# A static list schedule that counts the SBUF port of VectorE and GpSimd once, in a two-layer encoder kernel

## The chip, the cores and the metric

The kernel runs on one core of one Trainium2 chip. The metric is device time in microseconds (us); the kernel before takes 1868.65 us, the median of three runs (1866.95 to 1869.14).

## The reference

Two inputs, `x_prompt` (512 tokens) and `x_sample` (256 tokens), both 1024 wide, go through two layers of the same trunk. Cut to what matters:

```python
for l in range(2):
    h = rms_norm(x, norm_mix[l]);  proj = h @ w_in[l]          # q: 16 heads, k and v: 8 heads, 64 wide
    o_a = dense attention, 4 heads, axial rotary positions
    o_b = neighbourhood attention, 6 heads: a query sees up to 8 rows x 16 columns of the token grid,
          with a learned bias per head
    o_c = dilated attention, 6 heads, three branches merged by their softmax sums
    y = concat(rms_norm(o_a), rms_norm(o_b), rms_norm(o_c)) * out_gain[l]
    x = x + y @ w_out[l]
    gate, up = split(rms_norm(x, norm_ffn[l]) @ w_gate_up[l])  # 2 x 2816 wide
    x = x + (silu(gate) * up) @ w_down[l]
```

## The kernel before, in words

All 768 tokens stay in SBUF, feature-major, as blocks of 128. `p` counts three pairs of blocks: 0 and 1 are the prompt, 2 is the sample. Every float32 operand of a large product is split into a rounded part (`wh`, `Tph`, ...) and the difference to it (`wl`, `Tpl`, ...); `mm3` (L498 to L500) then makes three matmuls in place of one. A weight piece (`Piece`) is loaded by SP into one of two `raw` tiles, rounded by ScalarE into `wh` (L473), and the difference goes to `wl` (L474). Which engine does the difference is said by the parameter `wlo`, which is `POOL` in both layers. There are four `wh`/`wl` pairs.

A layer has an attention stage and an FFN stage. In the attention stage, for each of eight head groups `g` (the three of the neighbourhood mixer, m = 1, come first, then the dilated ones, m = 2, then the dense ones, m = 0), `emit_qkv` makes q, k and v (norms and rotary positions are small elementwise work on DVE and POOL, L661 to L704; L712 and L716 transpose the result), and `emit_attn` does, for each pair of blocks and each of two heads: scores (L781), bias and minimum (L826), exponential (L829), transposes of the probabilities (L840), rounding (L865) and difference (L866) of the transposed probabilities, product with the values (L876), and evacuation (L885, L890). `emit_out` scales by the output norm (L938 to L941) and projects. The residual add is L965. `norm2` (with `root`, L504 to L523) and `split` (L529, L532) prepare the FFN.

In the neighbourhood mixer the prompt's probabilities lie in a tile of 384 columns, three blocks of keys. A block of queries uses 256 of these; the rest is set to zero by `pads` on POOL (L820, L822). All three key blocks are transposed, rounded and multiplied for both query blocks, the blocks of zeros too.

The order of the instructions on each engine is no hand-written list. Every operation is recorded in a `Plan` with an engine (or several to choose from), a cost in us and a priority; `Plan.emit` simulates the engines with these costs and writes the instructions out in the order that comes from it. Each engine then works its list strictly in order, so a late instruction holds up those behind it. Among several engines one is passed over when another would finish over `TOL` = 0.7 us sooner. Costs before: an elementwise operation of n columns takes 0.07 + n/960 on DVE and 0.155 + 0.0021 n on POOL, whatever the other of the two does; a matmul takes its columns over 2400. Waits are set from the data, so the costs change the order alone.

```python
        def start_time(o, e):
            s = max(clock[e], o.ready)
            ...
    ew(width, lambda E: E.tensor_tensor(self.flat(1), raw[0][:, :width], self.flat(0).bitcast(F32), op=OP.subtract),
       r=[raw] + w[0], w=w[1], prio=prio, on="wlo")
```

Of the kernel before, what the change touches and what calls it, by code (L numbers as in the profile page):

```python
# [8 lines left out]
F32 = mybir.dt.float32  # L9
# [31 lines left out]
     qw=-8.0, qp2=-1.0, wlo='POOL', sth='ACT', rot='DVE POOL', cos='DVE POOL', radd='POOL', qsc='DVE POOL',  # L41
     stl='DVE POOL', qcp='ACT', kcp0='DVE', kcp1='ACT', kcp2='ACT', bias='POOL', pth='ACT', ysq='POOL', yadd='POOL', alo='DVE',
     nsq='ACT', nadd='DVE', nhi='ACT DVE', nlo='POOL', yhl='DVE POOL', tout=0, tdn=1, n1=2, nf=86, gus=-1, sf=5, wide=(), om=1,
# [6 lines left out]
     qw=-8.0, qp2=0, wlo='POOL', sth='ACT', rot='POOL', cos='DVE POOL', radd='POOL', qsc='DVE POOL', stl='DVE POOL',  # L50
     qcp='ACT', kcp0='DVE', kcp1='ACT', kcp2='ACT', bias='DVE POOL', pth='ACT', ysq='POOL', yadd='POOL', alo='POOL', nsq='ACT',
     nadd='DVE POOL', nhi='ACT DVE', nlo='POOL', yhl='DVE POOL', tout=0, tdn=1, n1=2, nf=86, gus=-1, sf=5, wide=(), om=1,
# [20 lines left out]
class Op:  # L73
    __slots__ = ("eng", "cost", "fn", "prio", "ndep", "outs", "ready", "alloc", "bufs", "end", "lat", "start", "seq", "bytes", "opts", "rank")


class Plan:
# [36 lines left out]
    def op(self, eng, cost, fn, r=(), w=(), prio=0.0, after=(), lat=0.0, nbytes=0):  # L114
        o = Op()
        o.opts = {eng: (cost, fn)} if isinstance(eng, str) else {e: (c, f) for e, c, f in eng}
        o.eng = next(iter(o.opts))
        o.cost, o.fn = o.opts[o.eng]
        o.prio, o.lat, o.bytes = prio, lat, nbytes
        o.seq = len(self.ops)  # L120
        o.alloc, o.bufs, o.outs, o.ready = [], set(), [], 0.0
        deps = set(after)
        for t in list(r) + list(w):
            b = t if isinstance(t, Buf) else (t[0] if isinstance(t, tuple) and isinstance(t[0], Buf) else None)
            if b is not None and b not in o.bufs:
                o.bufs.add(b)
                b.left += 1
                if b.first is None:
                    b.first = o
                    o.alloc.append(b)  # L130
                else:
                    deps.add(b.first)
        for t in r:
            if t in self.writer:
                deps.add(self.writer[t])
            self.readers.setdefault(t, []).append(o)
        for t in w:
# [12 lines left out]

    def emit(self):
# [59 lines left out]
        while left:  # L211
# [24 lines left out]
            o.cost, o.fn = o.opts[e]  # L236
# [7 lines left out]
            o.start = s  # L244
            clock[o.eng] = s + o.cost
# [28 lines left out]
def trunk(ctx: ExitStack, tc: tile.TileContext, t):  # L274
# [96 lines left out]
    def dve(n, fn, r=(), w=(), prio=0.0, fast=False):  # L371
        return P.op("DVE", v_cost(n, fast), fn, r, w, prio, lat=0.05)
# [6 lines left out]
    def ew(n, fn, r=(), w=(), prio=0.0, on="DVE POOL", act=None, fast=False, ptr=False, sbuf=True, extra=0):  # L379
# [9 lines left out]
        return P.op(opts, 0.0, None, r, w, prio, lat=0.05)  # L389
# [7 lines left out]
    TR = 0.108  # L397
# [104 lines left out]
    def root(parts, n, prio, exact, rb, out, to):  # L502
# [6 lines left out]
        else:  # L509
# [4 lines left out]
                r=[tok, (sh, 0)], w=[(sh, 1)], prio=prio)  # L514
# [5 lines left out]
            pe(2 * 0.108, total, r=[(sh, 0), (sh, 1), "ones"], w=[pm, (rb, "hold")], prio=prio)  # L520
# [113 lines left out]
    def emit_qkv(l, g, bs, wp, gains, rope):  # L634
# [6 lines left out]
        for p in order(g):  # L641
            acc = P.buf("D")
            av = lambda acc=acc: acc[0].rearrange("p (j c) -> p j c", j=2)
            for j in range(2):
                for kk in range(0, KC, 2):
# [5 lines left out]
                    pe(6 * 0.108, mm, r=[x for x in pc[kk // 4].tokens if len(x) == 2 or x[2] == kk // 2 % 2] + [x for x in pc[1].tokens if kk == 0 and len(x) == 2] + [  # L651
# [67 lines left out]
            pe(4 * 0.056, trq, r=[(stk, 0), (stk, 1), "identr"], w=[pq], prio=pr)  # L719
            ew(512, lambda E, p=p, pq=pq: E.tensor_copy(query(gs, p), pq[0]), r=[pq], w=[(gs[p], "q", p)], prio=pr, on="qcp",  # L720
               act=lambda p=p, pq=pq: ACT.copy(query(gs, p), pq[0]), sbuf=False)
            pe(2 * 0.056, trk, r=[(stk, 0), (stk, 1), "identr"], w=[pk], prio=pr)
# [9 lines left out]
    def emit_attn(l, g, gs, bs, mc):  # L732
# [15 lines left out]
        for p in order(g):  # L748
# [11 lines left out]
            wide = (g, p) in K["wide"]  # L760
# [6 lines left out]
            for h in range(2):  # L767
                PP = []
                for j in range(2):
# [14 lines left out]
                    pe(2 * nk / 2400.0, qk, r=[(gs[p], "q", p)] + ktok, w=[S], prio=pr)  # L784
# [13 lines left out]
                    else:  # L798
# [33 lines left out]
                for c in range(0, nch, 2):  # L832
                    n = min(2, nch - c)
                    pt = P.buf("PT")

                    def tr(c=c, n=n, pt=pt, PP=PP):
                        v = pt[0].rearrange("p (c j t) -> p c j t", c=2, j=2)
                        for cc in range(n):
                            for j in range(2):
                                PE.transpose(v[:, cc, j], PP[j][0][:, (c + cc) * 128:(c + cc + 1) * 128], ident)  # L840

                    rr_ = PP + ([(a, 1) for a in PP] if m == 1 and p < 2 else [])
                    pe(2 * n * TR, tr, r=rr_ + ["ident"], w=[pt], prio=pr)
                    vt = [(gs[pp], "v", pp, i) for pp in ((0, 1) if p < 2 else (2,)) for i in range(2)]
                    if wide:
                        for cc in range(n):
                            sr = lambda cc=cc, pt=pt: pt[0][:, cc * 256:(cc + 1) * 256]
                            ds = lambda c=c, cc=cc, PP=PP: PP[cc][0][:, c * 128:c * 128 + 256]
                            ew(256, lambda E, sr=sr, ds=ds: E.tensor_copy(ds(), sr()), r=[pt], w=[(PP[cc], "t", c)], prio=pr,
                               sbuf=False, on="pth", act=lambda sr=sr, ds=ds: ACT.copy(ds(), sr()))  # L850

                        def pv(c=c, n=n, h=h, p=p, po=po, nch=nch, c0=c0, PP=PP):
                            for cc in range(n):
                                kb = c0 + c + cc
                                pp, jj = (kb // 2, kb % 2) if p < 2 else (2, c + cc)
                                v = vals(gs, pp)[:, jj].bitcast(F32)
                                PE.matmul(po[0][:, h * 256:(h + 1) * 256], v, PP[cc][0][:, c * 128:c * 128 + 256],
                                          start=c + cc == 0, stop=c + cc == nch - 1)

                        pe(4 * n * 0.108, pv, r=[(PP[cc], "t", c) for cc in range(n)] + vt, w=[po], prio=pr)  # L860
                        continue
                    ps_ = P.buf("PTS")
                    ew(256 * n, lambda E, n=n, pt=pt, ps_=ps_: E.tensor_copy(ps_[0][:, :256 * n], pt[0][:, :256 * n]), r=[pt],
                       w=[(ps_, 0)], prio=pr, sbuf=False, on="pth",
                       act=lambda n=n, pt=pt, ps_=ps_: ACT.copy(ps_[0][:, :256 * n], pt[0][:, :256 * n]))  # L865
                    dve(256 * n, lambda n=n, pt=pt, ps_=ps_: DVE.tensor_tensor(  # L866
                        ps_[1][:, :256 * n], pt[0][:, :256 * n], ps_[0][:, :256 * n].bitcast(F32), op=OP.subtract),
                        r=[pt, (ps_, 0)], w=[(ps_, 1)], prio=pr)

                    def pv(c=c, n=n, ps_=ps_, h=h, p=p, po=po, nch=nch, c0=c0):  # L870
                        for cc in range(n):
                            kb = c0 + c + cc
                            pp, jj = (kb // 2, kb % 2) if p < 2 else (2, c + cc)
                            v = vals(gs, pp)[:, jj]
                            for i in range(2):
                                PE.matmul(po[0][:, h * 256:(h + 1) * 256], v, ps_[i][:, cc * 256:(cc + 1) * 256],  # L876
                                          start=(c + cc == 0 and i == 0), stop=(c + cc == nch - 1 and i == 1))

                    pe(2 * n * 0.108, pv, r=[(ps_, 0), (ps_, 1)] + vt, w=[po], prio=pr)
# [33 lines left out]
    def emit_out(l, m, bs):  # L913
# [6 lines left out]
        for p in order(LAST[m]):  # L920
# [22 lines left out]
            for cp in range(4):  # L943
                acc = P.buf("D")
                for j in range(2):
# [7 lines left out]
                    pe(3 * n * 0.108, mm, r=[x for c in pc for x in c.tokens] + [(y, z) for y in yts for z in range(2)], w=[acc],  # L953
# [15 lines left out]
    def emit_ffn(l, base, ends, late):  # L969
        f0 = 0  # L970
        lastsilu = None
        for part, nf in enumerate(FPARTS):
            pb_ = base + part * 20
            ab = []
            for f in range(f0, f0 + nf):
# [9 lines left out]
                for s in ((1, 0) if K["gus"] < 0 and part == 0 and f < 2 else (0, 1)):  # L985
# [4 lines left out]
                    for u in range(2):  # L990
                        for kk in range(0, KC, 2):
# [5 lines left out]
                            pe(6 * n / 2400.0, mm, r=pc[kk // 4].tokens + [  # L997
# [31 lines left out]
            if part < len(FPARTS) - 1:  # L1029
                for c in range(KC):  # L1030
# [3 lines left out]
                    for s in range(2):  # L1034
                        n = 512 if s == 0 else 256
                        for i in range(nf):
# [4 lines left out]
                            pe(3 * n / 2400.0, mm, r=pc.tokens + [(ab[i], 0, s), (ab[i], 1, s)], w=[accs[s]], prio=pd)  # L1041
# [4 lines left out]
            else:  # L1046
# [4 lines left out]
                for p in range(3):  # L1051
                    s, o = (0, p * 256) if p < 2 else (1, 0)
                    for cp in range(4):
                        acc = P.buf("ANY")
                        for j in range(2):
# [5 lines left out]
                            pe(3 * nf * 0.108, mm, r=pcs[cp].tokens + [(a, z, s) for a in ab for z in range(2)], w=[acc],  # L1061
# [132 lines left out]
```

## Time and profile before

| | us |
|---|---|
| median of three runs | 1868.65 |
| the profiled execution, its own time | 1867.04 |
| its span, first to last instruction | 1865.3 |
| PE busy | 1803.0 |
| DVE busy | 817.3 |
| ACT busy | 767.0 |
| POOL busy | 830.7 |

The time outside the span is 1.7 us. Engines: PE is TensorE (PEld its weight loads), DVE VectorE, ACT ScalarE, POOL GpSimd, SP SyncE, which issues the DMAs. A matmul counts as busy from its issue to the modelled end, and matmuls overlap, so the rate of matmuls is read from the distances of their starts. The attention stages lie at about 47 to 403 us and 925 to 1326 us of the span, the FFN stages behind each of them.

### The profile page before, as it was taken

To read this page: it belongs to the slowest core of one execution; us is meant where nothing else is said; L and a number is where in the kernel's file an instruction comes from. 1 tells how busy PE (TensorE), PEld (TensorE's weight loads), DVE (VectorE), ACT (ScalarE), POOL (GpSimd) and SP (SyncE) were. 2 spreads that over 40 slices of the span, in tenths; PEclk is the share of its full clock that TensorE was granted. 3 is DMA by queue.
4 is the path that set the end of the run, shared out by engine and by line. 5 is a ranking of instruction groups with operands and counts; after the bars stand their busy time and mean duration, and the time that the engine had idled before them with its cause. 6 is when DMAs were issued, how large, how long until landed. Compare 5 with 4: busy or idle time off the path is not lost.

```text
span 1865.3 us, 30054 instructions
## 1 busy us (share of the span) xinstructions
PE 1803.0 (97%) x12008; PEld 1648.0 (88%) x12008; DVE 817.3 (44%) x1678; ACT 767.0 (41%) x1738; POOL 830.7 (45%) x711
## 2 busy tenths in 40 slices
PE   6999999989999999999998999998999999999999
PEld 5998999878888888888998999998888888888889
DVE  8788678762111211211668876877411111111112
ACT  5887586642112212212457765866421122122120
POOL 4775354343333433433435653543454354355342
PEclk8999999999999999999998999999999999999999
DMA  4321111112211221122222211101212222122212
GB/s 147 84 57 46 35 44 37 35 46 63 63 60 66 60 76 57 55 73 67 69 59 59 61 35 35 53 24 35 68 49 66 68 63 60 60 68 60 69 58 86
DMA packets 56892, 110.61 MB, mean 59 GB/s; under 512 B 24496, under 2 KB 29616, under 8 KB 56752
## 3 DMA queue, kind: packets, MB, share of 16 engines
q1 hardware_dynamic: 56752, 108.69, 19.0%
q8 instruction: 94, 1.54, 0.3%
q14 instruction: 46, 0.38, 0.1%
HBM read 105.52 MB, written 3.15 MB: 58 GB/s over the span
## 4 chain that ended last, share of the span: by engine, by line
PE 84%; DVE 9%; ACT 3%; issue 2%; DMA 1%; POOL 1%; SPq 0%; DVEq 0%; POOLq 0%; ACTq 0%
PE ps L498 25%; PE ps L499 25%; PE ps L500 25%; PE ps L876 3%; PE ps L781 3%; PE ps L840 2%; DVE Tpl L532 1%; PE ps L712 1%; DVE rp L866 1%; DVE stk L704 1%; DVE y L938 1%; ACT wh L473 0%; DVE p L826 0%; DVE Tsl L532 0%; PE ps L902 0%
## 5 line engine op out<-in xcount | busy, mean ns | idle before, releaser
L474 POOL TENSOR_TENSOR wl<-raw,wh 128x1024 fp32r<-128x1024 f32 (+1 forms) x186 | 421.4, 2268 | 557.2 <-ACT wh L473 556.3
L473 ACT CAST wh<-raw 128x1024 fp32r<-128x1024 f32 (+1 forms) x186 | 184.4, 992 | 510.7 <-PE ps L499 499.7
L499 PE MATMUL ps<-Tpl,wh 128*128 128x512 f32 x704 | 278.4, 395 | 1.1 <-DVE Tpl L532 1.1
L498 PE MATMUL ps<-Tph,wh 128*128 128x512 f32 x704 | 278.5, 396 | 0.0
L500 PE MATMUL ps<-Tph,wl 128*128 128x512 f32 x704 | 274.1, 389 | 0.0
L500 PE MATMUL ps<-Tsh,wl 128*128 128x256 f32 x704 | 199.4, 283 | 0.0
L499 PE MATMUL ps<-Tsl,wh 128*128 128x256 f32 x704 | 199.2, 283 | 0.0
L498 PE MATMUL ps<-Tsh,wh 128*128 128x256 f32 x704 | 198.3, 282 | 0.0
L1004 DVE TENSOR_TENSOR p<-ps,bt 128x256 f32<-128x256 f32 x88 | 35.9, 420 | 344.5 <-PE ps L500 331.2
L498 PE MATMUL ps<-wh,Tph 128*128 128x256 f32 x512 | 152.1, 297 | 9.6 <-ACT wh L469 8.8
L500 PEld LDWEIGHTS ps<-Tph,wl 128*128 128x128 f32 x704 | 132.6, 188 | 30.2
L499 PE MATMUL ps<-wl,Tph 128*128 128x256 f32 x512 | 146.9, 287 | 3.0 <-DVE wl L470 2.9
L498 PEld LDWEIGHTS ps<-Tph,wh 128*128 128x128 f32 x704 | 133.8, 190 | 17.7
L499 PEld LDWEIGHTS ps<-Tpl,wh 128*128 128x128 f32 x704 | 133.8, 190 | 16.7 <-DVE Tpl L532 1.4
L500 PE MATMUL ps<-wh,Tpl 128*128 128x256 f32 x512 | 146.4, 286 | 0.0
L498 PEld LDWEIGHTS ps<-Tsh,wh 128*128 128x128 f32 x704 | 133.9, 190 | 14.1
L499 PEld LDWEIGHTS ps<-Tsl,wh 128*128 128x128 f32 x704 | 133.9, 190 | 12.6
L1009 POOL TENSOR_TENSOR p<-p,p 128x512 f32<-128x512 f32 (+1 forms) x88 | 89.4, 1016 | 105.9 <-DVE p L1004 89.3
L1004 DVE TENSOR_TENSOR p<-ps,cs 128x512 f32<-128x512 f32 x88 | 60.4, 687 | 169.6 <-PE ps L500 169.1
L500 PEld LDWEIGHTS ps<-Tsh,wl 128*128 128x128 f32 x704 | 133.9, 190 | 0.0
L498 PE MATMUL ps<-yt,wh 128*128 128x256 f32 (+1 forms) x448 | 132.3, 295 | 0.0
L499 PE MATMUL ps<-yt,wh 128*128 128x256 f32 (+1 forms) x448 | 130.6, 292 | 0.9 <-DVE yt L941 0.8
(243 smaller groups left out, 4542.6 us busy)
## 6 DMA issues: line engine op xcount, KB each, us to landing
raw<-in_w_gu SPq DMA_DIRECT2D x88, 512.0 KB, 3.6
raw<-in_w_down SPq DMA_DIRECT2D x48, 384.0 KB, 3.1
raw<-in_w_in SPq DMA_DIRECT2D x32, 512.0 KB, 3.8
raw<-in_w_out SPq DMA_DIRECT2D x16, 512.0 KB, 3.8
raw<-in_w_down SPq DMA_DIRECT2D x8, 512.0 KB, 3.6
tbm<-in_rpb SPq DMA_DIRECT2D x96, 24.0 KB, 2.2
tbm<-in_rpb SPq DMA_DIRECT2D x48, 48.0 KB, 2.3
out_y<-xp SPq DMA_DIRECT2D x8, 256.0 KB, 2.1
```

The costliest lines, as they stand in the source:

```text
L473: act(width, lambda: ACT.copy(self.flat(0), raw[0][:, :width]), r=[raw], w=w[0], prio=prio)
L474: ew(width, lambda E: E.tensor_tensor(self.flat(1), raw[0][:, :width], self.flat(0).bitcast(F32), op=OP.subtract), r=[raw] + w[0], w=w[1], ...
L498: PE.matmul(out, a[0], b[0], start=start, stop=False)
L499: PE.matmul(out, a[0], b[1], start=False, stop=False)
L500: PE.matmul(out, a[1], b[0], start=False, stop=stop)
L532: ew(256, lambda E, k=k, g=g, p=p: E.scalar_tensor_tensor(tT(p, 1)[:, k], xT(p)[:, k], g, tT(p, 0)[:, k].bitcast(F32), op0=OP.mult, op1=OP ...
L704: ew(384, lambda E, rv=rv, stk=stk: E.tensor_tensor(stk[0][:, :, 1], rv(), stk[0][:, :, 0].bitcast(F32), op=OP.subtract), r=[(A, 1), (stk, ...
L781: PE.matmul(S[0][:, :nk], q, kk[:, k0:k0 + nk], start=i == 0, stop=i == 1)
L840: PE.transpose(v[:, cc, j], PP[j][0][:, (c + cc) * 128:(c + cc + 1) * 128], ident)
L876: PE.matmul(po[0][:, h * 256:(h + 1) * 256], v, ps_[i][:, cc * 256:(cc + 1) * 256], start=(c + cc == 0 and i == 0), stop=(c + cc == nch - ...
L1004: dve(n, lambda n=n, u=u, s=s, sg=sg, view=view: DVE.tensor_tensor(sg[u][:, :n], view(u), late[s][0][:, :n], op=OP.mult), r=[accs[u % len( ...
L1009: ew(n, lambda E, n=n, sg=sg: E.tensor_tensor(sg[1][:, :n], sg[0][:, :n], sg[1][:, :n], op=OP.mult), r=[(sg, 0)], w=[(sg, 1), sg], prio=pb ...
```

## The change

- `Plan.emit` keeps the time to which DVE and POOL hold a common port. A POOL operation starts no earlier than the port is free of DVE; a DVE operation marked `lock` (its operands all in SBUF) no earlier than the port is free of POOL. Both book it for their own cost. Operations of `ew` are marked by `sbuf`, one more in `root` by hand; a DVE operation that reads PSUM is not marked.
- The planned times of matmuls change: 0.0135 us is added to n/2400, 0.120 stands for 256 columns, 0.109 for a float32 transpose and 0.067 for a rounded one.
- `wlo` becomes `POOL DVE`: either engine may make a weight difference.
- In the neighbourhood mixer, prompt pairs, the key block that holds zeros alone for one query block is left out for that block (`grps`): one transpose, half of a rounding, half of a difference, and half the columns of two matmuls fewer for each head and pair. One of the three memsets goes with it; the others' priority falls by 1.
- A variant that no layer used (`wide`) is removed.

```diff
-     qw=-8.0, qp2=-1.0, wlo='POOL', sth='ACT', ...
+     qw=-8.0, qp2=-1.0, wlo='POOL DVE', sth='ACT', ...
...
+        port = {"DVE": 0.0, "POOL": 0.0}
+
+        def held(o, e):
+
+            if e == "POOL":
+                return port["DVE"]
+            return port["POOL"] if e == "DVE" and o.lock else 0.0
+
         def start_time(o, e):
-            s = max(clock[e], o.ready)
+            s = max(clock[e], o.ready, held(o, e))
...
             o.start = s
+            o.cost = o.opts[e][0]
+            if e == "POOL" or (e == "DVE" and o.lock):
+                port[e] = s + o.cost
...
-        return P.op(opts, 0.0, None, r, w, prio, lat=0.05)
+        return P.op(opts, 0.0, None, r, w, prio, lat=0.05, lock=sbuf)
...
-    TR = 0.108
+    TR = 0.109
...
-                    pe(6 * 0.108, mm, r=...)
+                    pe(6 * 0.120, mm, r=...)
...
+                        if p < 2 and p != j:
                             def pads(pr_=pr_, w0=w0, nk=nk, ncols=ncols):
-                                if w0 > 0:
-                                    POOL.memset(pr_[0][:, 0:w0], 0.0)
-                                if w0 + nk < ncols:
-                                    POOL.memset(pr_[0][:, w0 + nk:ncols], 0.0)
-
-                            P.op("POOL", 0.2, pads, r=[(gs[p], "q", p)], w=[(pr_, 1)], prio=pr - 1, lat=0.05)
+                                POOL.memset(pr_[0][:, 0:w0], 0.0)
+                                POOL.memset(pr_[0][:, w0 + nk:ncols], 0.0)
+
+                            P.op("POOL", 0.3, pads, r=[(gs[p], "q", p)], w=[(pr_, 1)], prio=pr, lat=0.05)
...
+                grps = [((c, c + 1), (0, 1)) for c in range(0, nch - 1, 2)]
+                if m == 1 and p < 2:
+                    grps = [((p, p + 1), (0, 1)), ((2 - 2 * p,), (1 - p,))]
+                for gi, (cs, js) in enumerate(grps):
+                    n = 128 * len(cs) * len(js)
...
+                    def pv(cs=cs, js=js, ps_=ps_, ...):
+                        wd = 128 * len(js)
+                        o = h * 256 + js[0] * 128
...
+                                PE.matmul(po[0][:, o:o + wd], v, ps_[i][:, z * wd:(z + 1) * wd], ...)
```

## Rows read from the trace of the kernel before

**Rows 1.** Busy time by stage: us, then busy (count) of each engine, granted clock.

```profile
core 0: us, PE busy (x) PEld busy (x) DVE busy (x) ACT busy (x) POOL busy (x), PEclk, DMA share, GB/s
0.00:47.00 47.00, 28.89 (x182) 27.93 (x183) 37.86 (x64) 24.38 (x57) 19.84 (x24) 0.89 0.44 147
47.00:403.00 356.00, 336.90 (x2685) 323.34 (x2684) 276.31 (x601) 247.94 (x652) 191.90 (x213) 0.99 0.17 49
403.00:925.00 522.00, 521.88 (x3021) 459.69 (x3019) 115.04 (x201) 118.72 (x175) 195.08 (x113) 1.00 0.21 64
925.00:1326.00 401.00, 379.87 (x2982) 363.59 (x2983) 307.81 (x666) 265.46 (x696) 187.39 (x207) 0.98 0.15 44
```

**Rows 2.** Waits of PE, whole span: us in total, times, longest.

```profile
PE ps L567 <- ACT yt L558: 6.2, 2, 5.7
...
PE ps L712 <- DVE stk L704: 3.7, 4, 1.2
...
PE ps L781 <- DVE g1a L726: 2.5, 1, 2.5
```

**Rows 3.** Timeline of POOL and DVE, 39 to 47 us: start, us, instruction.

```profile
39.55 0.56 DVE L704 TENSOR_TENSOR stk<-ppa,stk 128x384 fp32r<-128x384 f32 x1 [0.24 <-ACT stk L703]
...
45.77 2.39 POOL L474 TENSOR_TENSOR wl<-raw,wh 128x1024 fp32r<-128x1024 f32 x1 [4.33 <-ACT wh L473]
...
46.13 2.44 DVE L704 TENSOR_TENSOR stk<-ppa,stk 128x384 fp32r<-128x384 f32 x1 [0.15 <-ACT stk L703]
```

**Rows 4.** Timeline around 400 us, end of layer 0's attention stage.

```profile
396.90 4.83 POOL L474 TENSOR_TENSOR wl<-raw,wh 128x1024 fp32r<-128x1024 f32 x2
...
397.42 2.12 DVE L513 TENSOR_TENSOR yt<-tbm,yt 128x256 fp32r<-128x256 f32 x1 [1.27 <-ACT yt L512]
...
402.07 0.58 PE L518 MATMUL ps<-yt,ones 128*128 128x256 f32 x1 [3.95 <-DVE yt L513]
```

**Rows 5.** Timeline of PE, POOL and DVE around 990 us, layer 1.

```profile
990.25 1.64 PE L876 MATMUL ps<-rp,g0b 128*128 128x256 f32 x4 [3.30 <-DVE y L890]
...
992.71 2.68 POOL L474 TENSOR_TENSOR wl<-raw,wh 128x1024 fp32r<-128x1024 f32 x1
...
993.09 2.68 DVE L810 TENSOR_TENSOR bt<-tbm,maskb 128x256 f32<-128x256 f32 x1
...
996.77 1.00 PE L876 MATMUL ps<-rp,g0b 128*128 128x256 f32 x3 [1.51 <-DVE rp L866]
```

**Rows 6.** Timeline of DVE and POOL, start of the kernel.

```profile
23.39 7.39 DVE L532 SCALAR_TENSOR_TENSOR Tsl<-xs,gcol,Tsh 128x256 fp32r<-128x256 f32 x5
...
25.61 4.89 POOL L474 TENSOR_TENSOR wl<-raw,wh 128x1024 fp32r<-128x1024 f32 x2 [0.58 <-ACT wh L473]
```

**Rows 7.** Busy time and granted clock behind four long waits (columns as in rows 1).

```profile
34.00:38.00 4.00, 3.41 (x15) 3.24 (x16) 3.83 (x9) 1.65 (x7) 1.45 (x2) 0.50 0.00 1
...
402.00:406.00 4.00, 3.93 (x13) 3.45 (x14) 0.35 (x2) 0.89 (x2) 0.00 (x0) 0.52 0.46 134
990.00:994.00 4.00, 3.67 (x15) 3.40 (x16) 3.97 (x11) 2.29 (x8) 2.81 (x4) 0.50 0.48 137
...
1075.00:1079.00 4.00, 3.79 (x14) 3.35 (x15) 2.79 (x9) 1.93 (x6) 2.06 (x3) 0.59 0.26 101
```

**Rows 8.** The chain of work in order of time: start, us, what.

```profile
65.08 0.44 PE ps L840 x4
```

**Rows 9.** Timeline of PE at 45 us: starts of matmuls of 256 and 128 columns.

```profile
45.04 0.28 PE L500 MATMUL ps<-wh,Tpl 128*128 128x256 f32 x1
45.16 0.29 PE L716 MATMUL ps<-identr,stk 128*128 128x128 f32 x2
45.28 0.35 PE L498 MATMUL ps<-wh,Tsh 128*128 128x256 f32 x1
```

**Rows 10.** Line L474 by stage: us, POOL busy (count), clock.

```profile
47.00:403.00 356.00, 61.23 (x26) 0.99 0.17 49
```

**Rows 11.** Timeline of DVE while POOL is idle: 512 and 256 columns.

```profile
32.31 0.68 DVE L544 TENSOR_TENSOR tbm<-tbm 128x512 f32<-128x512 f32 x1
32.91 0.41 DVE L555 TENSOR_TENSOR p<-p 128x256 f32<-128x256 f32 x1
```

More of the change, by code (lines that the diff above doesn't have):

```diff
@@ L40 @@
      q7=-3.5, a6=-4.0, a7=-1, o2=0.0, n2=0, w0=-20.0, qpost=-0.5, opost=-6.0, opc=0, qpc=-8.0, out=16.0, n0=-20.0, tpc=1.0,
-     qw=-8.0, qp2=-1.0, wlo='POOL', sth='ACT', rot='DVE POOL', cos='DVE POOL', radd='POOL', qsc='DVE POOL',
+     qw=-8.0, qp2=-1.0, wlo='POOL DVE', sth='ACT', rot='DVE POOL', cos='DVE POOL', radd='POOL', qsc='DVE POOL',
      stl='DVE POOL', qcp='ACT', kcp0='DVE', kcp1='ACT', kcp2='ACT', bias='POOL', pth='ACT', ysq='POOL', yadd='POOL', alo='DVE',
-     nsq='ACT', nadd='DVE', nhi='ACT DVE', nlo='POOL', yhl='DVE POOL', tout=0, tdn=1, n1=2, nf=86, gus=-1, sf=5, wide=(), om=1,
+     nsq='ACT', nadd='DVE', nhi='ACT DVE', nlo='POOL', yhl='DVE POOL', tout=0, tdn=1, n1=2, nf=86, gus=-1, sf=5, om=1,
      nsq0='ACT DVE', nadd0='DVE POOL', nhi0='ACT DVE', nlo0='POOL,DVE', nsq2='ACT,DVE', nadd2='DVE,POOL', nhi2='ACT',
@@ L49 @@
      q7=-1, a6=-4.0, a7=-1, o2=0.0, n2=0, w0=-20.0, qpost=-7.5, opost=-0.5, opc=-3, qpc=-8.0, out=16.0, n0=-20.0, tpc=1.0,
-     qw=-8.0, qp2=0, wlo='POOL', sth='ACT', rot='POOL', cos='DVE POOL', radd='POOL', qsc='DVE POOL', stl='DVE POOL',
+     qw=-8.0, qp2=0, wlo='POOL DVE', sth='ACT', rot='POOL', cos='DVE POOL', radd='POOL', qsc='DVE POOL', stl='DVE POOL',
      qcp='ACT', kcp0='DVE', kcp1='ACT', kcp2='ACT', bias='DVE POOL', pth='ACT', ysq='POOL', yadd='POOL', alo='POOL', nsq='ACT',
-     nadd='DVE POOL', nhi='ACT DVE', nlo='POOL', yhl='DVE POOL', tout=0, tdn=1, n1=2, nf=86, gus=-1, sf=5, wide=(), om=1,
+     nadd='DVE POOL', nhi='ACT DVE', nlo='POOL', yhl='DVE POOL', tout=0, tdn=1, n1=2, nf=86, gus=-1, sf=5, om=1,
      nsq0='ACT', nadd0='DVE POOL', nhi0='ACT', nlo0='POOL', nsq2='ACT,DVE', nadd2='DVE', nhi2='ACT', nlo2='POOL', qs=0.0,
@@ L73 @@
 class Op:
-    __slots__ = ("eng", "cost", "fn", "prio", "ndep", "outs", "ready", "alloc", "bufs", "end", "lat", "start", "seq", "bytes", "opts", "rank")
+    __slots__ = ("eng", "cost", "fn", "prio", "ndep", "outs", "ready", "alloc", "bufs", "end", "lat", "start", "seq", "bytes", "opts", "rank", "lock")
 class Plan:
@@ L112, in buf, with op @@
         return Buf(self, kind)
-    def op(self, eng, cost, fn, r=(), w=(), prio=0.0, after=(), lat=0.0, nbytes=0):
+    def op(self, eng, cost, fn, r=(), w=(), prio=0.0, after=(), lat=0.0, nbytes=0, lock=False):
         o = Op()
+        o.lock = lock
         o.opts = {eng: (cost, fn)} if isinstance(eng, str) else {e: (c, f) for e, c, f in eng}
@@ L235, in emit @@
             o.eng = e
-            o.cost, o.fn = o.opts[e]
+            o.fn = o.opts[e][1]
             if o.alloc:
@@ L369, in act, with dve @@
         return P.op("ACT", a_cost(n, sbuf, extra), fn, r, w, prio, after, lat=0.05)
-    def dve(n, fn, r=(), w=(), prio=0.0, fast=False):
-        return P.op("DVE", v_cost(n, fast), fn, r, w, prio, lat=0.05)
+    def dve(n, fn, r=(), w=(), prio=0.0, fast=False, lock=False):
+        return P.op("DVE", v_cost(n, fast), fn, r, w, prio, lat=0.05, lock=lock)
     def pool(n, fn, r=(), w=(), prio=0.0):
@@ L649, in mm @@
                             mm3(av()[:, j], [a[:, k] for a in hh], [a[:, k % 4] for a in pc[k // 4]()], k == 0, k == KC - 1)
[L651 removed]
+                    pe(6 * 0.120, mm, r=[x for x in pc[kk // 4].tokens if len(x) == 2 or x[2] == kk // 2 % 2] + [x for x in pc[1].tokens if kk == 0 and len(x) == 2] + [
                         ("T", p, k, i) for k in (kk, kk + 1) for i in range(2)],
@@ L831, in emit_attn @@
                         r=[mx, "table"], w=[pr_, (rsum, j, h)], prio=pr, extra=2)
[L832 to L843, printed above, removed]
-                    vt = [(gs[pp], "v", pp, i) for pp in ((0, 1) if p < 2 else (2,)) for i in range(2)]
[L845 to L863, printed above, removed]
@@ new lines, in emit_attn, with tr @@
+                grps = [((c, c + 1), (0, 1)) for c in range(0, nch - 1, 2)]
[3 more added lines that the diff above has]
+                    n = 128 * len(cs) * len(js)
+                    pt, ps_ = P.buf("PT"), P.buf("PTS")
+                    def tr(cs=cs, js=js, pt=pt, PP=PP):
+                        for i, (c, j) in enumerate([(c, j) for c in cs for j in js]):
+                            PE.transpose(pt[0][:, i * 128:(i + 1) * 128], PP[j][0][:, c * 128:(c + 1) * 128], ident)
+                    rr_ = [PP[j] for j in js] + [(PP[j], 1) for j in js if m == 1 and p < 2 and p != j]
+                    pe(n / 128 * TR, tr, r=rr_ + ["ident"], w=[pt], prio=pr)
+                    vt = [(gs[pp], "v", pp, i) for pp in ((0, 1) if p < 2 else (2,)) for i in range(2)]
+                    ew(n, lambda E, n=n, pt=pt, ps_=ps_: E.tensor_copy(ps_[0][:, :n], pt[0][:, :n]), r=[pt],
@@ L864, in emit_attn @@
                        w=[(ps_, 0)], prio=pr, sbuf=False, on="pth",
-                       act=lambda n=n, pt=pt, ps_=ps_: ACT.copy(ps_[0][:, :256 * n], pt[0][:, :256 * n]))
-                    dve(256 * n, lambda n=n, pt=pt, ps_=ps_: DVE.tensor_tensor(
-                        ps_[1][:, :256 * n], pt[0][:, :256 * n], ps_[0][:, :256 * n].bitcast(F32), op=OP.subtract),
+                       act=lambda n=n, pt=pt, ps_=ps_: ACT.copy(ps_[0][:, :n], pt[0][:, :n]))
+                    dve(n, lambda n=n, pt=pt, ps_=ps_: DVE.tensor_tensor(
+                        ps_[1][:, :n], pt[0][:, :n], ps_[0][:, :n].bitcast(F32), op=OP.subtract),
@@ L868, in emit_attn, with pv @@
                         r=[pt, (ps_, 0)], w=[(ps_, 1)], prio=pr)
[L870 to L873, printed above, removed]
+                    def pv(cs=cs, js=js, ps_=ps_, h=h, p=p, po=po, c0=c0, first=gi == 0, last=len(js) < 2 or gi == len(grps) - 1,
+                           more=gi < len(grps) - 1 and len(grps[gi + 1][1]) < 2):
+                        wd = 128 * len(js)
+                        o = h * 256 + js[0] * 128
+                        for z, c in enumerate(cs):
+                            kb = c0 + c
+                            pp, jj = (kb // 2, kb % 2) if p < 2 else (2, c)
@@ L874, in pv @@
                             v = vals(gs, pp)[:, jj]
                             for i in range(2):
-                                PE.matmul(po[0][:, h * 256:(h + 1) * 256], v, ps_[i][:, cc * 256:(cc + 1) * 256],
-                                          start=(c + cc == 0 and i == 0), stop=(c + cc == nch - 1 and i == 1))
-                    pe(2 * n * 0.108, pv, r=[(ps_, 0), (ps_, 1)] + vt, w=[po], prio=pr)
+                                end = z == len(cs) - 1 and i == 1
+                                PE.matmul(po[0][:, o:o + wd], v, ps_[i][:, z * wd:(z + 1) * wd],
+                                          start=first and z == 0 and i == 0, stop=end and (last or more),
+                                          **({} if wd > 128 else {"skip_group_check": True}))
@@ L951, in mm @@
                                 [yts[i][0][:, z * 256:(z + 1) * 256] for z in range(2)], i == 0, i == n - 1)
-                    pe(3 * n * 0.108, mm, r=[x for c in pc for x in c.tokens] + [(y, z) for y in yts for z in range(2)], w=[acc],
+                    pe(3 * n * 0.120, mm, r=[x for c in pc for x in c.tokens] + [(y, z) for y in yts for z in range(2)], w=[acc],
                        prio=bs[p])
@@ L1059, in mm @@
                                         [aap(i, s, z)[:, o:o + 256] for z in range(2)], i == 0, i == nf - 1)
-                            pe(3 * nf * 0.108, mm, r=pcs[cp].tokens + [(a, z, s) for a in ab for z in range(2)], w=[acc],
+                            pe(3 * nf * 0.120, mm, r=pcs[cp].tokens + [(a, z, s) for a in ab for z in range(2)], w=[acc],
                                prio=pd + p * 0.5)
```

16 lines of the change are left out of this document (8 added, 8 removed).

## The prediction

> **What bounds the kernel now.** I read the busy time by stage first, to see which engine sets each stage. PE does, nearly everywhere: in the FFN of layer 0 it is idle for 522.0 - 521.9 = 0.1 us, so nothing done there to DVE or POOL can give time back. The idle time of PE sits in the two attention stages, 356.0 - 336.9 = 19.1 and 401.0 - 379.9 = 21.1 us, and at the start, 47.0 - 28.9 = 18.1 us [rows 1]. In the attention stages DVE is busy 78% and 77%, POOL 54% and 47%. The question is who holds PE up there.
>
> The waits of PE name DVE or a chain that DVE feeds: 3.7 us in four waits for L704, 2.5 us in one wait for a key that DVE copied, 6.2 us at the start for a rounding that follows DVE sums [rows 2]. The timeline says why DVE is late. L704 takes 0.56 us when POOL is still; when POOL began a weight difference (2.39 us) just before it, it takes 2.44 us and ends 0.41 us after POOL does [rows 3]. At 396.9 us POOL makes two differences back to back, 4.83 us; DVE's L513 with 256 columns takes 2.12 us, and PE is idle 3.95 us for the differences of L513, until 0.34 us after POOL's end [rows 4]. At 992.7 us the same pair again: L474 2.68 us, L810 2.68 us, then PE idle 1.51 us, after an idle 3.30 us at 990 [rows 5]. At the start two differences of 4.89 us lie across five operations of L532 that take 7.39 us [rows 6]. So a DVE operation with two SBUF inputs does not run while a POOL operation runs; it waits for POOL's end.
>
> The Trainium skill, page "SBUF — State Buffer", section "Who interferes with whom", has the rule for this: a DVE instruction with two SBUF inputs blocks against a GpSimd one that reads SBUF. The rows agree (2.44 us against 0.56 us); the part of that rule that speaks against the change is a rival below.
>
> The long waits cost twice. Behind each the granted clock stands at about half: 0.50 at 34 us, 0.52 at 402, 0.50 at 990, 0.59 at 1075 [rows 7]; these stretches lie partly at 1.2 GHz, where 2.4 was granted before the wait.
>
> **The change, part by part.**
>
> *Half strips.* There are 3 groups x 2 prompt pairs x 2 heads x 2 layers = 24 cases. Each loses one transpose and 128 of 256 columns in two matmuls. Transposes start 0.44 / 4 = 0.11 us apart [rows 8]: 24 x 0.11 = 2.6 us. A matmul of 256 columns starts 0.12 us after the one before; two of 128 columns take (45.28 - 45.16) / 2 = 0.06 us each [rows 9]. 48 x 0.06 = 2.9 us. No product with 128 columns stands in the trace; the bounds are 0.06 (rounded transposes) and 0.11 (the full-precision transposes), so 48 x 0.01 = 0.5 to 2.9 us. I take 0.06, which has the same kind of operand. Sum 5.5 us (3.1 to 5.5), on the engine that bounds the stage.
>
> The Trainium skill, page "TensorE: Matmul & The Clock Gate", section "Wait — 56ns, not 53.3ns?", gives n/2.4 GHz + 2.5 ns, 55.6 ns for 128 columns. By that the matmuls would save 48 x 64 ns = 3.1 us and the part 5.7 us. The row's 0.12 us for 256 columns is above the page's rule, 109 ns, so I stay with rows.
>
> The halves of roundings and differences that go, on ACT and DVE, and the 24 memsets on POOL, are hidden behind PE's matmuls: I credit nothing. The remaining memsets come later by priority; no wait of PE names one, and if one fell behind a weight difference it could cost up to 2.4 us once.
>
> *Weight differences on either engine.* In the attention stages POOL makes 26 of them in layer 0, 61.23 / 26 = 2.36 us each [rows 10], and 27 in layer 1. On DVE, undisturbed, 512 columns take 0.68 us and 256 take 0.41 us [rows 11], so 1024 columns take about 0.68 + 2 x 0.27 = 1.22 us (at most twice the 512, 1.36). The planner counts DVE over 0.7 us sooner when both are free, so DVE will be chosen mostly. Then 53 x 1.22 = 65 us move onto DVE, the port is held for half as long, and DVE no longer stands still behind POOL. In the FFN stages the same move costs nothing: DVE is busy 115 of 522 us, and four weight pairs lie between a difference and its use; were that cover gone, each would cost up to 1.22 us of PE. SP's load of the next piece waits for the difference, which frees its `raw` tile; that comes about 1.1 us sooner from DVE, and no wait of PE names a load.
>
> *The port and the matmul times in the plan.* Nothing is added to the work; the order changes. Behind a weight difference DVE should now have operations that read PSUM, which run beside POOL, in place of one that stands still. What the new order is worth no row shows. From above it is bounded by the idle time behind blocked operations:
> - long waits in attention: 3.95 [rows 4] + 3.30 + 1.51 [rows 5] + 2.5 [rows 2] = 11.3 us, and the half clock behind them, busy PE time x (1 - clock): 3.93 x 0.48 + 3.67 x 0.50 + 3.79 x 0.41 = 5.3 us [rows 7]; together 16.6 us;
> - the waits for L704, 3.7 us;
> - the start, 6.2 us of wait [rows 2] and 3.41 x 0.50 = 1.7 us of clock; 7.9 us.
>
> From below, it may cost as much: a new order can set a stall of its own anywhere, and one long wait costs 4 us and its clock. I take half of the long waits, 8.3 us, because at 990 us DVE is busy 3.97 of 4 us [rows 7] and would have been late without the port too; two thirds of L704, 2.5 us, since those four are pure blocking; and at the start 3 us, little over the 4.89 - 2 x 1.22 = 2.4 us by which two differences are shorter on DVE.
>
> Sum: 5.5 + 8.3 + 2.5 + 3 = 19.3 us. The profiled execution took 1867.04 us (span 1865.3), so 1847.7 us; it lies 1.6 us under the median of the runs, 1868.65, so **1849 us**.
>
> **The rivals.**
>
> *Only the matmuls shrink.* The plan leaves differences on POOL where DVE's queue is full, or the blocking returns in other places. For it: DVE is near full where the stalls are [rows 7]. Against: four of four waits for L704 and the 3.95 us at 402 us are pure blocking. 1867.04 - 5.5 + 1.6 = 1863 us.
>
> *DVE becomes the bound (slower).* The place is the neighbourhood groups of layer 1, around 990 us, where DVE has no free time. A difference of 1.22 us ahead of an evacuation (L866, L890) holds PE directly. It decides from 19.3 / 1.22 = 16 of the 53 differences on PE's path; with 30 of them the time is 19.3 - 36.6 = 17 us over before, 1886 us. Against it: outside such places DVE has 80 and 93 us free, and stands still less.
>
> *All blocking goes.* 5.5 + 16.6 + 3.7 + 7.9 = 33.7 us: 1835 us. Against it: DVE's load at 990 us.
>
> *The plan locks too much.* It lets memsets hold the port like any POOL operation. If they don't on the chip, 48 planned holds of 0.3 us displace DVE work for nothing, up to 14.4 us if all were on the path: 1863 us. Nothing in the waits shows a memset that blocked. The Trainium skill, page "SBUF — State Buffer", section "Who interferes with whom", says that only a GpSimd instruction that reads SBUF blocks, not one that only writes.
>
> **How the numbers follow.** A difference under 0.2% (3.7 us) is about what cannot be told from no change. Chances: forecast 0.63 (its own range 1835 to 1858); only the matmuls 0.14, of which 0.10 is faster by over 0.2% and 0.04 within; all blocking or more 0.08; locks too much 0.04, half faster, half within; DVE the bound 0.11, slower. Faster 0.63 + 0.10 + 0.08 + 0.02 = 0.83, within 0.06, slower 0.11. The range goes down to 1829, since of PE's 40 us idle in attention I counted 15 us as blocked, and up to 1866 for the two rivals near 1863; what it leaves out is the slow rival and part of the fast one.
>
> **What would show it.** L840 should have 24 matmuls fewer, and the halved products be 0.06 us apart. L474 should stand mostly under DVE, near 1.2 us, in the FFN nearly wholly. L704, L513, L532 and L810 on DVE should lose their 2 us cases. The clock should stay whole at 402 and 1075 us; at the start PE's idle time should fall below 18.1 us. The FFN stages should keep their length. The prediction is wrong if PE's idle time in the attention stages stays near 40 us, if DVE's evacuations come later than before with DVE busy over 90%, or if a new wait of over 3 us drops the clock elsewhere.

## The result, and the profile after

The changed kernel takes 1836.54 us (median of four runs, 1836.17 to 1838.08) against 1868.22 us of four runs before: ratio 0.9832, 95% interval 0.9815 to 0.9849. The profiled execution took 1836.76 us, 30.3 us under that of before. The range given (1829 to 1866 us) holds it. The forecast of 1849 us gives 19.3 of the 31.7 us; the time stands next to the rival "all blocking goes", 1835 us.

From the page of the changed kernel: busy time of the engines, and the granted clock in 40 slices.

```profile
PE 1792.1 (98%) x11984; PEld 1638.9 (89%) x11984; DVE 934.1 (51%) x1835; ACT 765.4 (42%) x1745; POOL 479.1 (26%) x523
...
PEclk9999999999999999999999999999999999999999
```

The span fell by 1865.3 - 1835.0 = 30.3 us. PE's idle time in it fell from 62.3 to 1835.0 - 1792.1 = 42.9 us, which is 19.4 us; PE's busy time fell by 10.9 us. No slice of the 40 is under nine tenths of the clock. Summed over stretches of 2 us, busy PE time x (1 - clock) was 10.3 us before (7.2 of it behind the start) and is 1.7 us now, all of it at the start, at 28 to 32 us (last line below). The rows miss one stretch. They give a clock of 1.00 for the first 20 us of the kernel before and the first 25 us of the changed one, but there products of 256 columns start 0.22 us apart, as they do where the granted clock is 0.50, and not 0.12. Two lines of the kernel before, two of the changed one:

```profile
11.79 0.41 PE L500 MATMUL ps<-wh,Tpl 128*128 128x256 f32 x1
12.01 0.41 PE L498 MATMUL ps<-wh,Tph 128*128 128x256 f32 x1
...
19.38 0.41 PE L511 MATMUL ps<-wl,Tph 128*128 128x256 f32 x1
19.60 0.41 PE L512 MATMUL ps<-wh,Tpl 128*128 128x256 f32 x1
```

Half of PE's busy time there is 4.2 us before and 4.9 us now. So of the 10.9 us by which PE is less busy, about 8 are clock.

Busy time of the changed kernel by stage, columns as in [rows 1]; the stages start earlier, so the windows are moved with them. The next two lines answer to 402 and 990 us of [rows 7], the last shows where the half clock is left.

```profile
0.00:47.00 47.00, 29.59 (x191) 28.32 (x192) 33.37 (x70) 27.35 (x62) 8.51 (x10) 0.96 0.47 152
47.00:388.00 341.00, 332.44 (x2654) 319.53 (x2654) 269.33 (x615) 243.38 (x651) 151.60 (x189) 1.00 0.16 49
388.00:910.00 522.00, 522.00 (x3032) 460.05 (x3030) 180.44 (x267) 119.80 (x177) 68.40 (x50) 1.00 0.21 65
910.00:1296.00 386.00, 372.83 (x2970) 357.82 (x2969) 300.28 (x675) 265.50 (x698) 142.96 (x183) 1.00 0.16 48
...
402.00:406.00 4.00, 4.00 (x19) 3.34 (x18) 1.23 (x1) 0.34 (x1) 0.00 (x0) 1.00 0.35 101
988.00:992.00 4.00, 4.00 (x37) 4.00 (x36) 3.39 (x12) 3.91 (x15) 1.83 (x4) 1.00 0.40 100
...
28.00:32.00 4.00, 4.00 (x24) 4.00 (x23) 3.06 (x5) 1.68 (x4) 0.00 (x0) 0.57 0.17 33
```

The FFN stage of layer 0 keeps its 522 us with 65 us more on DVE: the cover there held. The attention stages are 15 us shorter each, 341 for 356 and 386 for 401 us. PE idles 8.6 us there in layer 0 (19.1 before) and 13.2 us in layer 1 (21.1 before).

Waits of PE in the changed kernel: us in total, times, longest.

```profile
PE ps L511 <- DVE wl L482: 5.0, 1, 5.0
PE ps L873 <- DVE rp L859: 4.2, 6, 1.2
...
PE ps L579 <- ACT yt L570: 1.6, 1, 1.6
...
PE ps L724 <- DVE stk L716: 0.4, 1, 0.4
```

The wait for `stk` (L704 before, L716 now) fell from 3.7 to 0.4 us, those for `yt` of ACT from 6.2 to 1.6 us [rows 2]. One at the start, for a difference of the first weights, grew from 2.9 us to 5.0; its line before:

```profile
PE ps L499 <- DVE wl L470: 2.9, 1, 2.9
```

Groups of the changed kernel, shapes apart: count | busy us, mean ns | idle before.

```profile
L486 DVE TENSOR_TENSOR wl<-raw,wh 128x1024 fp32r<-128x1024 f32 x124 | 154.5, 1246 | 129.7 <-ACT wh L485 129.5
...
L873 PE MATMUL ps<-rp,g1b 128*128 128x256 f32 x288 | 49.7, 293 | 3.0 <-DVE rp L859 2.5 <-DVE y L888 0.2
...
L486 POOL TENSOR_TENSOR wl<-raw,wh 128x1024 fp32r<-128x1024 f32 x14 | 35.3, 2526 | 56.8 <-ACT wh L485 56.8
...
L716 DVE TENSOR_TENSOR stk<-ppa,stk 128x384 fp32r<-128x384 f32 x32 | 19.0, 592 | 3.6 <-ACT stk L715 2.8
...
L873 PE MATMUL ps<-rp,g0b 128*128 128x128 f32 x32 | 6.4, 281 | 0.0
```

The weight differences of 1024 columns went to DVE, 124 of 138, at 1.25 us (1.22 had been forecast). `stk` on DVE takes 0.59 us on average, near the 0.56 us it takes undisturbed [rows 3].

### The profile page after: what moved, and what is told of

The parts are those of the page before. It is cut to its first block, busy times and chain, and to the rows that moved or that the text cites. A ratio compares the mean times of both kernels' runs of the same rounds, so it can differ in the third digit from the quotient of the medians.

```text
span 1835.0 us, 29851 instructions
## 1 busy us (share of the span) xinstructions
PE 1792.1 (98%) x11984; PEld 1638.9 (89%) x11984; DVE 934.1 (51%) x1835; ACT 765.4 (42%) x1745; POOL 479.1 (26%) x523
## 3 DMA queue, kind: packets, MB, share of 16 engines
q1 hardware_dynamic: 56752, 108.69, 19.3%
## 5 line engine op out<-in xcount | busy, mean ns | idle before, releaser
L1007 POOL TENSOR_TENSOR p<-p,p 128x512 f32<-128x512 f32 (+1 forms) x88 | 115.0, 1307 | 803.7 <-DVE p L1002 720.7
L486 DVE TENSOR_TENSOR wl<-raw,wh 128x1024 fp32r<-128x1024 f32 (+1 forms) x166 | 194.8, 1174 | 168.5 <-ACT wh L485 168.2
L512 PE MATMUL ps<-yt,wl 128*128 128x256 f32 (+1 forms) x448 | 130.1, 290 | 0.0
```

Source lines behind the costliest of these rows:

```text
L512: PE.matmul(out, a[1], b[0], start=False, stop=stop)
L1007: ew(n, lambda E, n=n, sg=sg: E.tensor_tensor(sg[1][:, :n], sg[0][:, :n], sg[1][:, :n], op=OP.mult), r=[(sg, 0)], w=[(sg, 1), sg], prio=pb ...
```

## The experiments

Each was timed in three rounds beside the kernel before on the same chip. Ratios are to those runs of before. PE idle is the span less PE's busy time in the one profiled execution.

| kernel | median us | ratio (95%) | PE idle us |
|---|---|---|---|
| changed kernel | 1836.54 | 0.9832 (0.9815 to 0.9849) | 42.9 |
| before + half strips | 1868.38 | 0.9994 (0.9985 to 1.0004) | 67.4 |
| before + one planned time | 1870.18 | 1.0007 (0.9997 to 1.0016) | 66.9 |
| before + port | 1845.54 | 0.9875 (0.9860 to 0.9890) | 50.1 |
| before + either engine | 1854.79 | 0.9919 (0.9905 to 0.9934) | 53.6 |
| before + matmul times | 1892.03 | 1.0124 (1.0109 to 1.0139) | 78.9 |
| changed - port | 1870.82 | 1.0011 (1.0001 to 1.0020) | 66.1 |
| changed - either engine | 1842.94 | 0.9858 (0.9844 to 0.9873) | 44.5 |
| changed - matmul times | 1836.09 | 0.9820 (0.9805 to 0.9834) | 43.8 |
| changed - half strips | 1843.57 | 0.9863 (0.9846 to 0.9879) | 44.5 |
| changed - port, slow DVE | 1861.77 | 0.9960 (0.9946 to 0.9974) | 61.5 |
| changed, memsets off the port | 1837.85 | 0.9834 (0.9819 to 0.9848) | 41.4 |
| changed, first differences free | 1835.41 | 0.9820 (0.9805 to 0.9834) | 41.4 |

"Before +" is the kernel before with one part of the change put in, "changed -" the changed kernel with one part taken out. Two theories stood against each other. *Engine*: most of the gain comes from the differences leaving POOL. *Order*: the plan has only to know when the port is held. The rival to both is that any new order moves the time. Against it stands the table as a whole: the seven versions whose plan knows of the port lie at 0.982 to 0.988 of the time before, the six whose plan does not at 0.992 to 1.012, the kernel before at 1, and each version has an order of its own.

**Before + half strips.**

```diff
...
+                if m == 1 and p < 2:
+                    grps = [((p, p + 1), (0, 1)), ((2 - 2 * p,), (1 - p,))]
...
```

The change to the memsets and to their priority goes with it.

> The kernel before with the half strips alone (the plan's costs and the engine of the weight differences stay as before). If each matmul of 128 columns takes 0.06 us, as the prediction had it, 5.5 us faster, about 1863 us. If it takes 0.115 us, as the changed kernel's trace has it, only the 24 transposes count: 2.6 us faster, about 1866 us. If what counts is that any edit draws a new order, the time moves by more than that, either way.

1868.38 us, no difference that can be told. The 2.6 us of work lie inside the interval; 5.5 us do not. The run alone does not settle the size, though: in the profiled execution PE is busy 4.9 us less than before and idle 5.1 us more, so the new order took back what the work gave. The lines on L873 below do settle it.

**Before + port in the plan.**

```diff
...
-            s = max(clock[e], o.ready)
+            s = max(clock[e], o.ready, held(o, e))
...
```

> The kernel before with the port in the plan alone; weight differences stay on POOL. Theory of the engine (most of the gain comes from the differences leaving POOL): 5 to 12 us faster, DVE operations with two SBUF inputs still held up to 2.4 us. Theory of the order (the plan only has to know of the port): 20 us or more faster.

1.25% or 23 us faster, as the theory of the order has it, though all 186 differences still go to POOL. The plan also chooses anew where either engine may do an operation, but little moved: DVE has 1657 instructions for 1678 before, POOL 720 for 711. DVE is busy 775.6 us, for 817.3 before: 21 instructions fewer, of 0.49 us on average, are some 10 of these 41.7 us; the rest is time in which it stood still.

```profile
PE 1793.7 (97%) x12008; PEld 1642.5 (89%) x12008; DVE 775.6 (42%) x1657; ACT 770.4 (42%) x1750; POOL 831.5 (45%) x720
```

The timeline of this kernel, POOL and DVE, shows what the plan does with one of them.

```profile
172.53 2.41 POOL L486 TENSOR_TENSOR wl<-raw,wh 128x1024 fp32r<-128x1024 f32 x1 [0.49 <-ACT wh L485]
...
172.97 0.69 DVE L878 TENSOR_TENSOR rp<-ps,rp 128x512 fp32r<-128x512 f32 x1
173.58 0.41 DVE L838 CUSTOM_DVE_ANT_0 p<-ps,tbm 128x256 f32<-128x256 f32 x1
...
173.95 0.69 DVE L878 TENSOR_TENSOR rp<-ps,rp 128x512 fp32r<-128x512 f32 x1
174.56 0.41 DVE L838 CUSTOM_DVE_ANT_0 p<-ps,tbm 128x256 f32<-128x256 f32 x1
```

While POOL works its 2.41 us, DVE makes four operations that read PSUM (`ps`) at their plain times. In [rows 3] and [rows 4] it stood still in such a stretch.

**Before + either engine.**

```diff
-     ... wlo='POOL', ...
+     ... wlo='POOL DVE', ...
```

> The kernel before with the weight differences on either engine alone; the plan does not know of the port. Theory of the engine: 10 to 18 us faster, most differences on DVE at 1.2 us, the DVE operations held over 2 us gone, no half clock at 402 us. Theory of the order: within 4 us of before.

0.81% or 15 us faster, as the theory of the engine has it; that of the order, within 4 us, misses here. But of the long waits not all went. Waits of PE in this kernel, with two lines of its timeline, then in the one with the port alone:

```profile
PE ps L876 <- DVE y L890: 7.2, 6, 3.3
```

```profile
974.92 2.37 POOL L474 TENSOR_TENSOR wl<-raw,wh 128x1024 fp32r<-128x1024 f32 x1
...
979.83 1.64 PE L876 MATMUL ps<-rp,g0b 128*128 128x256 f32 x4 [3.30 <-DVE y L890]
```

```profile
PE ps L888 <- DVE y L902: 2.9, 3, 1.4
```

The longest of the first is the wait at 990 us [rows 5], 3.3 us still: 60 of the 186 differences stayed on POOL, and one of 2.37 us lies ahead of this wait as before. With the port in the plan the longest is 1.4 us. That does not show that the port alone can take this wait away: in "changed - port" the longest of this kind is 1.6 us, and other waits stand in its place.

**Before + measured matmul times.**

```diff
-    TR = 0.108
+    TR = 0.109
...
-                    pe(6 * 0.108, mm, ...)
+                    pe(6 * 0.120, mm, ...)
...
```

> The kernel before with the measured matmul times in the plan alone. Both theories: within 5 us of before, as no work changes. If a new order by itself moves the time, up to 10 us either way.

1.24% or 23 us slower, which neither theory had, nor the rival of the new order with its 10 us. The waits of PE in this kernel, and its timeline at one of them:

```profile
PE ps L712 <- DVE stk L704: 9.3, 6, 2.9
...
PE ps L518 <- DVE yt L513: 8.9, 3, 4.6
```

```profile
141.54 5.03 POOL L474 TENSOR_TENSOR wl<-raw,wh 128x1024 fp32r<-128x1024 f32 x2
...
141.70 2.64 DVE L698 TENSOR_TENSOR ppa<-ppa,sm 128x384 f32<-128x384 f32 x1
...
145.72 1.28 DVE L704 TENSOR_TENSOR stk<-ppa,stk 128x384 fp32r<-128x384 f32 x1
...
147.05 0.53 PE L712 MATMUL ps<-identr,stk 128*128 128x128 f32 x4 [1.01 <-DVE stk L704]
```

They are waits for the same lines as in [rows 2] and [rows 4], 3.7 and 3.95 us there, grown to more than twice the time. At 141 us two differences on POOL hold first L698 and then L704, which ends 0.43 us after POOL does: the same blocking, and here PE waits for it.

**Changed - port in the plan.**

```diff
...
-            s = max(clock[e], o.ready, held(o, e))
+            s = max(clock[e], o.ready)
...
```

> The changed kernel, but the plan does not look at the port (differences on either engine, measured matmul times and half strips stay). If what the parts give alone simply adds up, 23 us slower than the changed kernel, about 1860 us. If the measured matmul times do harm only while the plan takes DVE and POOL for independent, more than that is lost: 1860 to 1885 us, with DVE held 25 us or more in each attention stage.

1870.82 us: the whole gain is lost, 0.9832 to 1.0011, more than the 23 us of the port alone. The other three edits together give nothing without it. If each elementwise operation on DVE is set against the shortest tenth of its like, DVE is held some 34 us in each attention stage here, by this estimate, against 16 us in the changed kernel and 40 before. Waits of PE in this kernel:

```profile
PE ps L510 <- DVE vs L678: 6.1, 2, 5.8
...
PE ps L724 <- DVE stk L716: 4.4, 5, 2.2
```

**Changed - either engine** (`wlo='POOL'`).

> The changed kernel with all weight differences on POOL. Theory of the engine (a difference on POOL holds DVE whatever the order): 10 to 15 us slower, 1847 to 1852 us, some 25 DVE operations held behind differences. Theory of the order (the plan that knows of the port steps round them): within 4 us of the changed kernel.

0.9858 against 0.9832: 0.26% or 5 us slower by the ratios, between the two forecasts and near that of the order. The two intervals overlap, so the size is rough.

**Changed - matmul times** (0.108 for 256 columns and so on).

> The changed kernel with the matmul times of before in the plan (the four query transposes keep the new one; with all of them old the plan finds no order). If the measured times do harm by themselves, as in the kernel before, 10 to 20 us faster than the changed kernel, about 1820 us. If they help once DVE and POOL are planned rightly, 5 us or more slower, 1842 us and up.

0.9820 against 0.9832: no difference, which neither forecast had. What cost 23 us without the port costs nothing with it.

**Changed - half strips.**

```diff
-                    grps = [((p, p + 1), (0, 1)), ((2 - 2 * p,), (1 - p,))]
+                    grps = [((0, 1), (0, 1)), ((2,), (0, 1))]
```

> The changed kernel with the blocks of zeros transposed, split and multiplied again. By the trace of the changed kernel (transposes 0.11 us, 128 columns 0.115 against 0.120 us for 256) 24 x 0.11 + 48 x 0.005 = 2.9 us slower, about 1839 us; by the prediction's 0.06 us 5.5 us slower, 1842 us; over 8 us either way would be the redrawn order.

(The third memset comes back with them.) 0.9863 against 0.9832: 0.31% or 6 us slower, of which the work explains 2.9; where the rest comes from was not followed, and the intervals overlap.

**Changed - port, slow DVE.** Is it the exclusive hold, or would a plan do that takes DVE for slower?

```diff
...
-        cost = {"DVE": v_cost(n, fast, ptr), ...
+        cost = {"DVE": v_cost(n, fast, ptr) + (0.26 if sbuf else 0.0), ...
```

> The changed kernel without the port in the plan, but each DVE operation that reads SBUF alone is planned 0.26 us longer, about what such an operation lost on average in the kernel before. Theory of the port (the plan must know when POOL holds the port): it stays near the version without the port, 1860 to 1875 us. Rival (the plan only had to take DVE for slower): most of the gain is back, 1845 us or less.

1861.77 us: 1.0011 to 0.9960, 0.5%, of the 1.8% that the port is worth. A plan that takes DVE for slower by this much (no other length was tried) does not do; the plan has to know when POOL holds the port.

**Changed, memsets off the port.**

```diff
-                return port["DVE"]
+                return port["DVE"] if o.lock else 0.0
...
-            if e == "POOL" or (e == "DVE" and o.lock):
+            if o.lock and e in port:
```

> The changed kernel with the memsets taken out of the plan's port: they neither wait for DVE nor hold it up. If the chip lets a memset run beside DVE, the plan is nearer to it: 0 to 5 us faster than the changed kernel, and no DVE operation held behind a memset. If memsets do hold the port, DVE operations held behind them appear and it is 2 us or more slower.

0.9834 against 0.9832: no difference. The traces say why: a memset neither waits for DVE nor holds it. In the changed kernel, POOL and DVE:

```profile
54.62 0.60 DVE L716 TENSOR_TENSOR stk<-ppa,stk 128x384 fp32r<-128x384 f32 x1 [0.47 <-ACT stk L715]
...
54.74 0.15 POOL L831 MEMSET p<- 128x64 f32 x1
...
55.00 0.15 POOL L832 MEMSET p<- 128x64 f32 x1
```

Four memsets begin while L716 runs, the last at 55.00; each takes 0.15 us and L716 its usual 0.60. So the plan sets time aside for them that the chip does not need, and that costs nothing that can be told.

**Changed, first differences free.**

```diff
-     ... w0d='DVE,POOL', ...
+     ... w0d='DVE POOL', ...
```

> The changed kernel with the weight differences of the very first pieces on either engine instead of DVE and POOL in turn. In the changed kernel the second one on POOL takes 3.70 us, held behind DVE, and PE is idle 4.96 us at the start behind these differences. If that holding is the cause, 3 to 6 us faster than the changed kernel, 1831 to 1834 us; if the start is bound by DVE's load anyway, within 2 us.

0.9820 against 0.9832: no difference that can be told, within 2 us. The wait of PE at the start did get shorter, 3.4 us for 5.0 in the waits of this kernel:

```profile
PE ps L511 <- DVE wl L482: 3.4, 1, 3.4
```

That shorter wait does not show in the time.

**Before + one planned time** (`TR = 0.109`).

> The kernel before with one planned time changed, that of a transpose, from 0.108 to 0.109 us; no work changes, but the order does. It measures what a redrawn order alone is worth while the plan does not know of the port. If the 23 us of the measured matmul times are such a redraw, this too can move by 5 us or more, either way; if they are an effect of the times themselves, it stays within 4 us of before.

1.0007, no difference. So the 23 us of the matmul times are more than this one redrawn order makes; it is one draw, and a larger redraw was not tried.

No version beats the changed kernel: the best two, 1835.41 and 1836.09 us, lie within its interval.

## Why the prediction was right, and where not

*What bounds the kernel* was right. The time came back in the attention stages, from PE's waits and the lower clock behind them; DVE held by POOL was their cause. The experiment that takes the port out of the plan shows it: time, PE's idle time (66.1 us) and the waits for `stk` (4.4 us) come back. Of the terms, the 6.2 us of wait at the start were 5.7 us; the rest of that line stands at 925 us.

*Half strips* was mis-sized: 5.5 us taken, 2.8 found. The choice of 0.06 us for a product of 128 columns was the wrong bound. Three lines of the changed kernel's PE timeline:

```profile
57.45 0.29 PE L728 MATMUL ps<-identr,stk 128*128 128x128 f32 x2
57.58 0.41 PE L873 MATMUL ps<-rp,g0b 128*128 128x128 f32 x2
57.82 0.73 PE L851 MATMUL ps<-identr,p 128*128 128x128 f32 x5
```

Two transposes of 128 columns are over in 57.58 - 57.45 = 0.13 us, two products of 128 columns in 57.82 - 57.58 = 0.24 us, 0.12 us each, as long as one of 256. Over all 48 such products the mean is 0.117 us (leaving out one behind which PE waits); in 6 of the 24 pairs the first is over in 0.06 us, in the others it takes 0.13 to 0.14. The row that I took for "the same kind" is another kind, so a product of 128 columns saves next to nothing. A nearer row stood in the trace of the kernel before: L567 multiplies rounded operands with 2 columns only, and at the full clock four of these products take 43.65 - 43.28 = 0.37 us, 0.11 us apart behind the first.

```profile
43.28 0.50 PE L567 MATMUL ps<-ones,yt 128*128 128x2 f32 x4
43.65 0.36 PE L498 MATMUL ps<-wh,Tsh 128*128 128x256 f32 x1
```

So below 256 columns the number of columns is not what sets the time of these products; what does, the load of the weights perhaps, no run shows. The Trainium skill, page "TensorE: Matmul & The Clock Gate", section "Wait — 56ns, not 53.3ns?", gives 55.6 ns for 128 columns. These lines do not bear that out for rounded products; the measurement decides. Only the transposes count, 2.6 us, and the kernel with half strips alone shows no gain.

*Weight differences on either engine* was right in what moves (53 in the attention stages forecast, 40 of 52 on DVE found, 50.9 us or 1.27 us each) and that FFN hides it. As the main lever it was not: alone it gives 15 us, but with the port planned only some 5 us. The theory of the engine, with which I went into the experiments, falls. The gains do not add up, so the two edits must in part take the same stalls away.

*The port in the plan* was the step that I could not price, and its half was too little. Of the long waits (16.6 us with their clock) I took 8.3; all went: behind the start no wait of PE is over 1.6 us and the clock stands at 1.00. My reason was that DVE at 990 us had no free time. In part it had none because it stood still: of the 2.68 us of L810 some 2.1 are such time, since two of L810 together take 1.09 us a little later:

```profile
997.31 1.09 DVE L810 TENSOR_TENSOR bt<-tbm,maskb 128x256 f32<-128x256 f32 x2
```

In the whole stage DVE is now busy 300.3 of 386 us with 27 us of differences added, where it was 307.8 of 401 us. Waits for L704: 2.5 taken, 3.3 found. Start: 3 taken, about 1 found. PE starts 191 matmuls in the first 47 us where it started 182, and its idle time there fell only from 18.1 to 17.4 us; the granted clock of that stretch, 0.96 for 0.89, leaves out the first 20 to 25 us. With 2.8 us of half strips these make 16.6 + 3.3 + 1 + 2.8 = 23.7 of the 30.3 us. Read the other way, from the totals, the sum closes: 19.4 us less idle time, about 8 us of clock and 2.8 us of half strips are about 30 us. So what I had left uncounted is short waits, and some more half clock around 990 us than the three stretches of [rows 7] hold.

*The rivals.* "DVE becomes the bound" did not come. "All blocking goes" came nearest. "Locks too much" fell: freeing the memsets changes nothing. Its sum was too high besides: the plan has 24 such operations of 0.3 us, each with two memsets, so 7.2 us and not 14.4. The four memsets beside L716 are as the last sentence on that rival says. "Only the matmuls shrink" fell too.

*Not foreseen*: the measured matmul times cost 23 us when they come without the port. That a plan with too short times for all engines was at least balanced, and that lengthening PE alone makes it leave DVE's work until too late, would fit, and a slower DVE in the plan did give back a part; it was argued and not shown.

## What to carry to other kernels

When VectorE waits behind GpSimd, look first at what VectorE could do meanwhile: work that reads PSUM runs beside GpSimd, and putting it there gave 23 us with every weight difference left on GpSimd. A planner's costs are best corrected together; one group of them made right alone made this kernel slower. Before counting a halved matmul as half the time, find one of that shape and kind in a trace.

## What the runs showed of the hardware that was not expected

A rounded product (`fp32r`) of 128 columns occupies PE nearly as long as one of 256, 0.117 us on average against 0.12, and one of 2 columns 0.11 us, where the rounded transposes of L728 with 128 columns take 0.06 us. A memset on POOL runs beside a DVE operation with two SBUF inputs, 0.15 us each within the 0.60 us of L716. And the hold works both ways. From the changed kernel's timeline, DVE and POOL, and one of its groups:

```profile
379.93 2.34 DVE L486 TENSOR_TENSOR wl<-raw,wh 128x1024 fp32r<-128x1024 f32 x2
...
380.15 3.28 POOL L556 TENSOR_TENSOR p<-p,p 128x512 f32<-128x512 f32 x1 [4.81 <-ACT p L554]
```

```profile
L1007 POOL TENSOR_TENSOR p<-p,p 128x512 f32<-128x512 f32 x44 | 56.9, 1293 | 532.5 <-DVE p L1002 519.3 <-ACT wh L485 13.2
```

POOL's L556 with 512 columns takes 3.28 us behind two differences on DVE and ends 1.16 us after they do. The same shape of operation takes 1.29 us on average in the FFN (L1007), where DVE has little to do.
